# A weighted copy of 16384 token rows: 126 tokens per partition in large tiles, 256 tokens in a small tile

## The chip, the cores and the metric

The kernel runs on one core of one Trainium2 chip. The metric is the device time of one execution in microseconds; of the kernel before three runs are given. Besides, one execution was taken with the hardware profiler. Four of the core's engines matter here: VectorE (DVE in the profile) and ScalarE (ACT) compute, SyncE (SP) issues transfers, and ScalarE issues transfers too. The transfers of both are carried out by the core's sixteen DMA engines. Data lie in HBM; the on-chip memory has 128 partitions.

## The reference

Each of 16 x 1024 = 16384 tokens has a row of 512 float32 numbers and two weights. The output has two rows per token, the token's row times each weight. The expert indices are not used.

```python
batch, seq, hidden, n_experts = 16, 1024, 512, 8
k = 2

x_expanded = x[:, :, np.newaxis, :].repeat(k, axis=2)
weights = expert_weights[..., np.newaxis]
return (x_expanded * weights).astype(np.float32)
```

So 33.6 MB are read and 67.1 MB written, and each output number costs one multiplication.

## The kernel before

The tokens are dealt to 128 partitions, 128 tokens per partition, in six groups of 24, 24, 24, 24, 16 and 16 tokens per partition. Within a group each partition holds that many consecutive tokens, so that what one partition loads is one contiguous run of HBM (24 x 2 KB = 48 KB), and so is what it stores of one half group (12 x 4 KB = 48 KB).

The weights of all tokens come first, in three transfers issued by SP (line 59). A group of x is one load issued by ScalarE (`load`, line 90); the first group is loaded in six steps of 4, 4, 4, 6, 4 and 2 tokens. There are two buffers for x and two for the output. The output of a group is made in two halves; each half has a buffer of its own and one store, issued by SP (line 143).

In the first half of the first group the products are single: one instruction multiplies one row of 512 numbers in each of the 128 partitions by that partition's weight. Every third goes to ScalarE (line 110), the others to VectorE (line 116). In all other halves VectorE works in blocks of six tokens: one instruction (line 127) makes the eight rows of four tokens (or four rows where two tokens are left), with the x row repeated and the weight spread over 512 numbers, and ScalarE makes the four rows of the other two tokens singly.

What sets the order: each engine works through its instructions in order and waits on semaphores. The load of group i + 2 is issued by ScalarE after its products of group i, since it takes the buffer of group i and VectorE must also have finished with it. A half's products wait until the store that last used the output buffer (two halves earlier) has landed. The stores stand in SP's queue in the order of the halves.

Of the kernel before, what the change touches and what calls it, by code (L numbers as in the profile page):

```python
# [1 line left out]

# [4 lines left out]


@with_exitstack
def kernel(  # L10
    ctx: ExitStack,
    tc: tile.TileContext,
    x: bass.AP,
    expert_indices: bass.AP,
    expert_weights: bass.AP,
    out: bass.AP,
):
    nc = tc.nc

    batch, seq, hidden = x.shape  # L20
    k = expert_weights.shape[-1]
    P = nc.NUM_PARTITIONS
    ntok = batch * seq
    assert ntok % P == 0
    A_TOTAL = ntok // P

    f32 = mybir.dt.float32
    row = k * hidden
    TX = 24
    TO = 12  # L30
    CH = 4

    groups = [[24], [24], [24], [24], [16], [16]]
    assert sum(sum(g) for g in groups) == A_TOTAL

    xf = x.rearrange("b s h -> (b s) h")
    of = out.rearrange("b s k h -> (b s) (k h)")
    wf = expert_weights.rearrange("b s k -> (b s) k")

    w_pool = ctx.enter_context(tc.tile_pool(name="w_pool", bufs=1))  # L40
    x_pool = ctx.enter_context(tc.tile_pool(name="x_pool", bufs=2))
    o_pool = ctx.enter_context(tc.tile_pool(name="o_pool", bufs=2))

    w_tile = w_pool.tile([P, A_TOTAL * k], f32)

    def rows(of_all, done, T):
        return of_all[done * P : (done + T) * P, :].rearrange(
            "(p a) n -> p (a n)", a=T
        )

    runs = [[sum(groups[0]), 1]]
    for T in [sum(g) for g in groups[1:]]:
        if len(runs) > 1 and runs[-1][0] == T:
            runs[-1][1] += 1
        else:
            runs.append([T, 1])
    head = 0
    for T, G in runs:
        nc.sync.dma_start(
            out=w_tile[:, head * k : (head + G * T) * k].rearrange(  # L60
                "p (g n) -> p g n", g=G
            ),
            in_=wf[head * P : (head + G * T) * P, :].rearrange(
                "(g p a) n -> p g (a n)", g=G, p=P
            ),
        )
        head += G * T

    tiles = []
    done = 0  # L70
    for group in groups:
        T = sum(group)
        a0 = 0
        for n in group:
            tiles.append((done, T, a0, n))
            a0 += n
        done += T

    loaded = []

    def load(i):
        if i >= len(tiles):
            return
        done, T, a0, n = tiles[i]
        x_tile = x_pool.tile([P, TX * hidden], f32)
        src = rows(xf, done, T)
        steps = [4, 4, 4, 6, 4, 2] if i == 0 else [n]
        for e, step in enumerate(steps):
            at = sum(steps[:e])
            nc.scalar.dma_start(  # L90
                out=x_tile[:, at * hidden : (at + step) * hidden],
                in_=src[:, (a0 + at) * hidden : (a0 + at + step) * hidden],
            )
        loaded.append(x_tile)

    for i in range(2):
        load(i)
    for i, (done, T, a0, n) in enumerate(tiles):
        x_tile = loaded[i]
        outr = rows(of, done, T)  # L100
        half = n // 2
        for t in range(n):
            if t % half == 0:
                o_tile = o_pool.tile([P, TO * row], f32)
            single = i == 0 and t < half
            for kk in range(k if single or t % half % 6 > 3 else 0):
                c = (done + a0 + t) * k + kk
                o = t % half * row + kk * hidden
                if not single or c % 3 == 2:
                    nc.scalar.mul(  # L110
                        out=o_tile[:, o : o + hidden],
                        in_=x_tile[:, t * hidden : (t + 1) * hidden],
                        mul=w_tile[:, c : c + 1],
                    )
                    continue
                nc.vector.tensor_scalar(  # L116
                    out=o_tile[:, o : o + hidden],
                    in0=x_tile[:, t * hidden : (t + 1) * hidden],
                    scalar1=w_tile[:, c : c + 1],
                    scalar2=None,  # L120
                    op0=mybir.AluOpType.mult,
                )
            if not single and t % half % 6 == 0:
                c = (done + a0 + t) * k
                o = t % half * row
                m = min(CH, half - t % half)
                nc.vector.tensor_tensor(  # L127
                    out=o_tile[:, o : o + m * row].rearrange(
                        "p (t k h) -> p t k h", t=m, k=k
                    ),  # L130
                    in0=x_tile[:, t * hidden : (t + m) * hidden]
                    .rearrange("p (t h) -> p t h", t=m)
                    .unsqueeze(2)
                    .to_broadcast([P, m, k, hidden]),
                    in1=w_tile[:, c : c + m * k]
                    .rearrange("p (t k) -> p t k", t=m)
                    .unsqueeze(3)
                    .to_broadcast([P, m, k, hidden]),
                    op=mybir.AluOpType.mult,
                )  # L140
            if (t + 1) % half == 0:
                at = t // half * half
                nc.sync.dma_start(  # L143
                    out=outr[:, (a0 + at) * row : (a0 + t + 1) * row],
                    in_=o_tile[:, : (t + 1 - at) * row],
                )
        load(i + 2)

# [1 line left out]
_INS = ['x', 'expert_indices', 'expert_weights']  # L150
_OUTS = [((16, 1024, 2, 512), 'float32')]


# [23 lines left out]
```

## Time and profile before

| | |
|---|---|
| three runs | 239.81, 242.17, 242.68 us (median 242.17) |
| profiled execution | span 240.7 us; the page lists no other time for it |
| VectorE busy | 94.5 us, 38 instructions |
| ScalarE busy | 51.8 us, 81 instructions |
| moved by DMA | 100.80 MB, mean 419 GB/s |
| chain that ended last | DMA 76%, VectorE 12% of the span |

The span goes from the first to the last instruction. Stretches of the span are given with the busy time of each engine in them, the share of the sixteen DMA engines' time that was used, and the GB/s moved. A share of 1.00 means that all sixteen were busy; one engine of sixteen is 0.06. The queue q1 is SP's (weights and stores), q10 ScalarE's (loads of x), and q14 brings instructions.

### The profile page before, as it was taken

How to read it: one execution, taken by the hardware profiler on the slowest of the kernel's cores; microseconds unless marked ns; L12 is line 12 of the kernel's file. 1: busy time of each engine (PE TensorE's matmuls, PEld its weight loads, DVE VectorE, ACT ScalarE, POOL GpSimd, SP SyncE). 2: the span in 40 equal slices, each digit the busy share in tenths (PEclk: the TensorE clock that was granted, in tenths of full speed). 3: DMA queues.
4: the chain of work that ended last, by engine and by line, in shares of the span. 5: the costliest groups of instructions: out<-in, count | busy, mean ns of one | idle time of the engine just before them, and what ended most of it. 6: DMA issues, size and time to landing. Idle time of an engine off the chain costs nothing.

```text
span 240.7 us, 231 instructions
## 1 busy us (share of the span) xinstructions
DVE 94.5 (39%) x38; ACT 51.8 (22%) x81; POOL 0.2 (0%) x4
## 2 busy tenths in 40 slices
DVE  0879000002979000391067093019346005594700
ACT  0860030002553000350071170016040004043000
POOL 0000000000000000000000000000000000000000
DMA  7999999999999999999999999999999999899994
GB/s 257 427 405 451 431 404 408 498 392 408 506 392 400 515 392 392 515 402 392 482 433 392 449 436 436 436 403 490 400 427 436 427 397 438 359 436 436 436 436 180
DMA packets 4129, 100.80 MB, mean 419 GB/s; under 512 B 1184, under 2 KB 1184, under 8 KB 1312
## 3 DMA queue, kind: packets, MB, share of 16 engines
q1 hardware_dynamic: 2544, 67.24, 64.9%
q10 hardware_dynamic: 1584, 33.56, 32.9%
q14 instruction: 1, 0.01, 0.0%
HBM read 33.69 MB, written 67.11 MB: 419 GB/s over the span
## 4 chain that ended last, share of the span: by engine, by line
DMA 76%; DVE 12%; issue 4%; DVEq 1%; ACT 1%; SPq 0%; ACTq 0%
DMA out_dram<-o_tile 63%; DMA x_tile<-in_x_dram 14%; DVE o_tile L127 12%; DVEq L172 1%; ACT o_tile L110 1%; DVEq L127 0%; SPq L143 0%; ACTq L90 0%
## 5 line engine op out<-in xcount | busy, mean ns | idle before, releaser
L127 DVE TENSOR_TENSOR o_tile<-x_tile,w_tile 128x4096 f32<-128x4096 f32 (+1 forms) x22 | 87.9, 4034 | 126.0 <-DMA out_dram<-o_tile 89.5
L110 ACT ACTIVATE o_tile<-x_tile,w_tile 128x512 f32<-128x512 f32 x80 | 50.5, 709 | 164.6 <-DMA out_dram<-o_tile 124.4
L116 DVE TENSOR_SCALAR o_tile<-x_tile,w_tile 128x512 f32<-128x512 f32 x16 | 6.6, 481 | 6.7 <-DMA x_tile<-in_x_dram 6.7
L110 ACT ACT_TABLE_LOAD x1 | 1.3, 1283 | 6.7 <-DMA x_tile<-in_x_dram 6.7
L161 POOL MEMSET const-uint8-127<- 128x1 uint8 x1 | 0.1, 103 | 0.0
L161 POOL MEMSET const-bfloat16-1.0<- 128x1 bf16 x1 | 0.1, 102 | 0.0
L161 POOL MEMSET const-float32-0.0<- 128x1 f32 x1 | 0.1, 99 | 0.2 <-issue 0.2
L161 POOL MEMSET const-float32-1.0<- 128x1 f32 x1 | 0.1, 99 | 0.0
## 6 DMA issues: line engine op xcount, KB each, us to landing
out_dram<-o_tile SPq DMA_DIRECT2D x8, 6144.0 KB, 30.8
x_tile<-in_x_dram ACTq DMA_DIRECT2D x3, 6144.0 KB, 49.3
out_dram<-o_tile SPq DMA_DIRECT2D x4, 4096.0 KB, 12.5
x_tile<-in_x_dram ACTq DMA_DIRECT2D x2, 4096.0 KB, 29.0
x_tile<-in_x_dram ACTq DMA_DIRECT2D x4, 1024.0 KB, 8.6
x_tile<-in_x_dram ACTq DMA_DIRECT2D x1, 1536.0 KB, 12.8
x_tile<-in_x_dram ACTq DMA_DIRECT2D x1, 512.0 KB, 27.8
w_tile<-in_expert_weights_dram SPq DMA_DIRECT2D x1, 72.0 KB, 10.3
```

Source lines behind the costliest of these rows:

```text
L110: nc.scalar.mul(out=o_tile[:, o : o + hidden], in_=x_tile[:, t * hidden : (t + 1) * hidden], mul=w_tile[:, c : c + 1],)
L116: nc.vector.tensor_scalar(out=o_tile[:, o : o + hidden], in0=x_tile[:, t * hidden : (t + 1) * hidden], scalar1=w_tile[:, c : c + 1], scala ...
L127: nc.vector.tensor_tensor(out=o_tile[:, o : o + m * row].rearrange("p (t k h) -> p t k h", t=m, k=k), in0=x_tile[:, t * hidden : (t + m) * ...
L161: nc = _bacc.Bacc("TRN2", target_bir_lowering=False, num_devices=1)
L172: with _tile.TileContext(nc) as tc:
```

## The change

The first 256 tokens are taken out of the large tiles. The other 16128 are 126 per partition, in groups of 22, 22, 22, 22, 19 and 19; the halves have 11 and 11, or 10 and 9 tokens. A buffer for x holds 22 tokens, one for the output 11.

The 256 tokens lie in a small tile of their own. 240 of them fill partitions 32 to 91, four consecutive tokens in each, by one transfer of 60 partitions. The last 16 lie in a fifth place, in every fourth partition from 32 to 92, by one transfer of 16 partitions. This holds for their weights, for x and for the output. Their products are made on partitions 32 to 63 and 64 to 91 in turn (in the fifth place on 32 to 63 and 64 to 95, whose unused partitions two memsets have filled with zeros).

All products are single, two thirds of them on VectorE (line 112 of the new kernel) and a third on ScalarE (line 110). The small tile is loaded first, computed first and stored first. The first group's load has two parts, with the 16-partition load between them; only the first group's weights come through SP, the others through ScalarE's queue behind the first group's load. The program's order is the order in which the code stands (`manual_schedule`).

```diff
-    groups = [[24], [24], [24], [24], [16], [16]]
+    groups = [22, 22, 22, 22, 19, 19]
+    A_MAIN = sum(groups)
+    P0, NP, BAND = 32, 60, 4
+    NQ, STEP = 16, 4
+    n_band = NP * BAND
+    n_extra = n_band + NQ
...
+    def sides(t, n):
+        return (
+            t[P0 : P0 + NP, 0 : BAND * n],
+            t[P0 : P0 + NQ * STEP : STEP, BAND * n : (BAND + 1) * n],
+        )
...
+    nc.vector.memset(ew_tile[:, BAND * k :], 0.0)
+    nc.vector.memset(ex_tile[:, BAND * hidden :], 0.0)
...
+    def share(n):
+        return nc.scalar if n % 3 == 2 else nc.vector
+
+    a, b = sides(ew_tile, k)
+    nc.sync.dma_start(out=a, in_=band(wf, k))
+    nc.sync.dma_start(out=b, in_=ones(wf))
+    weights(nc.sync, 0, 1, groups[0])
+    a, b = sides(ex_tile, hidden)
+    nc.scalar.dma_start(out=a, in_=band(xf, hidden))
+    load(0, 0, 2)
+    nc.scalar.dma_start(out=b, in_=ones(xf))
+    load(0, 1, 2)
+    weights(nc.scalar, starts[1], 3, 22)
+    weights(nc.scalar, starts[4], 2, 19)
+    load(1)
+
+    for t in range(BAND + 1):
+        for p in (slice(32, 64), slice(64, P0 + NP if t < BAND else 96)):
+            for kk in range(k):
+                c = t * k + kk
+                product(share(c), p, eo_tile, c, ex_tile, t, ew_tile, c)
+    a, b = sides(eo_tile, row)
+    nc.sync.dma_start(out=band(of, row), in_=a)
+    nc.sync.dma_start(out=ones(of), in_=b)
+
+    for i, T in enumerate(groups):
...
+        for n in (T - T // 2, T // 2):
+            o_tile = o_pool.tile([P, TO * row], f32)
+            for c in range(n * k):
+                product(
...
-                nc.vector.tensor_tensor(
...
+            nc.sync.dma_start(
+                out=outr[:, at * row : (at + n) * row], in_=o_tile[:, : n * row]
+            )
+            at += n
         load(i + 2)
```

More of the change, by code (lines that the diff above doesn't have):

```diff
@@ L24 @@
     assert ntok % P == 0
-    A_TOTAL = ntok // P
     f32 = mybir.dt.float32
     row = k * hidden
-    TX = 24
-    TO = 12
-    CH = 4
-    groups = [[24], [24], [24], [24], [16], [16]]
-    assert sum(sum(g) for g in groups) == A_TOTAL
+    TX = 22
+    TO = 11
+    groups = [22, 22, 22, 22, 19, 19]
[4 more added lines that the diff above has]
+    n_extra = n_band + NQ
+    assert n_extra + A_MAIN * P == ntok
     xf = x.rearrange("b s h -> (b s) h")
@@ L40, with band, ones, rows @@
     w_pool = ctx.enter_context(tc.tile_pool(name="w_pool", bufs=1))
+    e_pool = ctx.enter_context(tc.tile_pool(name="e_pool", bufs=1))
     x_pool = ctx.enter_context(tc.tile_pool(name="x_pool", bufs=2))
     o_pool = ctx.enter_context(tc.tile_pool(name="o_pool", bufs=2))
-    w_tile = w_pool.tile([P, A_TOTAL * k], f32)
-    def rows(of_all, done, T):
-        return of_all[done * P : (done + T) * P, :].rearrange(
+    w_tile = w_pool.tile([P, A_MAIN * k], f32)
+    ew_tile = w_pool.tile([P, (BAND + 1) * k], f32)
+    ex_tile = e_pool.tile([P, (BAND + 1) * hidden], f32)
+    eo_tile = e_pool.tile([P, (BAND + 1) * row], f32)
+    def band(flat, n):
+        return flat[0:n_band, :].rearrange("(p a) n -> p (a n)", a=BAND)
+    def ones(flat):
+        return flat[n_band:n_extra, :]
+    def sides(t, n):
[3 more added lines that the diff above has]
+        )
+    def rows(flat, done, T):
+        return flat[n_extra + done * P : n_extra + (done + T) * P, :].rearrange(
             "(p a) n -> p (a n)", a=T
         )
[L51 to L59, printed above, removed]
+    def weights(eng, head, G, T):
+        lo = n_extra + head * P
+        eng.dma_start(
             out=w_tile[:, head * k : (head + G * T) * k].rearrange(
@@ L62 @@
             ),
-            in_=wf[head * P : (head + G * T) * P, :].rearrange(
+            in_=wf[lo : lo + G * T * P, :].rearrange(
                 "(g p a) n -> p g (a n)", g=G, p=P
@@ L66, with load @@
         )
[L67 to L77, printed above, removed]
+    ctx.enter_context(tc.manual_schedule())
+    nc.vector.memset(ew_tile[:, BAND * k :], 0.0)
+    nc.vector.memset(ex_tile[:, BAND * hidden :], 0.0)
+    starts = [sum(groups[:i]) for i in range(len(groups))]
     loaded = []
-    def load(i):
-        if i >= len(tiles):
+    def load(i, part=0, parts=1):
+        if i >= len(groups):
@@ L83, in load @@
             return
[L84 to L92, printed above, removed]
-            )
-        loaded.append(x_tile)
-    for i in range(2):
-        load(i)
@@ L98 @@
-    for i, (done, T, a0, n) in enumerate(tiles):
-        x_tile = loaded[i]
[L100 to L121, printed above, removed]
-                )
[L123 to L146, printed above, removed]
@@ new lines, in load, with product @@
+        T = groups[i]
+        if part == 0:
+            x_tile = x_pool.tile([P, TX * hidden], f32)
+            loaded.append(x_tile)
+        lo, hi = T * part // parts, T * (part + 1) // parts
+        nc.scalar.dma_start(
+            out=loaded[i][:, lo * hidden : hi * hidden],
+            in_=rows(xf, starts[i], T)[:, lo * hidden : hi * hidden],
+        )
+    def product(engine, p, o_tile, o, x_tile, i, w, c):
+        dst = o_tile[p, o * hidden : (o + 1) * hidden]
+        src = x_tile[p, i * hidden : (i + 1) * hidden]
+        if engine is nc.scalar:
+            engine.mul(out=dst, in_=src, mul=w[p, c : c + 1])
+        else:
+            engine.tensor_scalar(
+                out=dst,
+                in0=src,
+                scalar1=w[p, c : c + 1],
+                scalar2=None,
+                op0=mybir.AluOpType.mult,
+            )
```

11 lines of the change are left out of this document (added).

## The prediction

> **What bounds the kernel now.** I read the page first: the engines' totals, the forty slices, the DMA queues.
>
> ```profile
> span 240.7 us, 231 instructions
> DVE 94.5 (39%) x38; ACT 51.8 (22%) x81; POOL 0.2 (0%) x4
> ...
> DMA  7999999999999999999999999999999999899994
> ...
> DMA packets 4129, 100.80 MB, mean 419 GB/s; under 512 B 1184, under 2 KB 1184, under 8 KB 1312
> ...
> q1 hardware_dynamic: 2544, 67.24, 64.9%
> q10 hardware_dynamic: 1584, 33.56, 32.9%
> q14 instruction: 1, 0.01, 0.0%
> ```
>
> VectorE is busy for 39% and ScalarE for 22%; the DMA row is 9 from the second slice to the last but one. The two queues together fill 64.9 + 32.9 = 97.8% of sixteen DMA engines' span, 235.4 us of 240.7. So 5.3 us per DMA engine, on the mean, are idle, and no change that moves the same 100.80 MB at the same rate can win more than those. The question is where the 5.3 us lie. For that I cut the span into stretches.
>
> ```profile
> core 0: us, DVE busy (x) ACT busy (x) POOL busy (x), PEclk, DMA share, GB/s
> 0.00:1.70 1.70, 0.00 (x0) 0.00 (x0) 0.20 (x4) 1.00 0.00 0
> 1.70:6.00 4.30, 0.14 (x1) 0.00 (x0) 0.00 (x0) 1.00 0.99 359
> 40.00:80.00 40.00, 17.52 (x4) 10.02 (x16) 0.00 (x0) 1.00 1.00 433
> 207.00:207.60 0.60, 0.60 (x1) 0.00 (x0) 0.00 (x0) 1.00 0.01 0
> 207.60:208.80 1.20, 0.25 (x1) 0.00 (x0) 0.00 (x0) 1.00 0.57 246
> 208.80:209.20 0.40, 0.00 (x0) 0.00 (x0) 0.00 (x0) 1.00 1.53 655
> 230.00:236.00 6.00, 0.00 (x0) 0.00 (x0) 0.00 (x0) 1.00 1.01 437
> 238.20:239.40 1.20, 0.00 (x0) 0.00 (x0) 0.00 (x0) 1.00 0.06 27
> 239.40:240.70 1.30, 0.00 (x0) 0.00 (x0) 0.00 (x0) 1.00 0.00 0
> ```
>
> A stretch counts a transfer's packets where they start, so very short stretches swing between 0 and over 1, and I read them as marks of when engines start something. There are four idle places. The first 1.70 us hold no packet. The last 1.30 us hold none either (the last landing and the end of the program). From 238.20 to 239.40 the share is 0.06, which is one engine of sixteen, at 27 GB/s, which is 433 / 16: **one DMA engine works alone for 1.2 us** after the other fifteen are done. And near 208 almost nothing starts, then a burst at 208.80. Its size by subtraction: of 235.4 us busy, 0.07 lie after 238.20; 1.70 to 238.20 is 236.5 us long and holds 235.3 busy, so 1.2 us on the mean are lost there, and I put them at 208, the one place where I see engines start together.
>
> The chain of waits and the timeline tell why that gap exists.
>
> ```profile
> 170.43 30.67 DMA out_dram<-o_tile
> 201.10 0.03 issue
> ...
> 207.91 12.55 DMA out_dram<-o_tile
> ```
>
> ```profile
> 201.22 6.63 DVE L127 TENSOR_TENSOR o_tile<-x_tile,w_tile 128x4096 f32<-128x4096 f32 x2 [16.74 <-DMA out_dram<-o_tile]
> 207.91 19.69 SPq L143 DMA_DIRECT2D out_dram<-o_tile  x3
> ```
>
> A store landed at 201.10 and gave its buffer back; VectorE refilled it in 6.63 us; the next store left at 207.91. Meanwhile a single store of 4096 KB was in flight, with no load beside it: 4.19 MB at 433 GB/s is 9.7 us. The cover is 9.7 us against 6.63 plus the delay until the store begins, and a store that lands late on one engine eats the rest. So both losses, at 208 and at the end, fit one engine that lags: by 1.2 us at the end, and by at most 1.2 + 1.2 = 2.4 us without the gap, in which it could catch up.
>
> **The change, part by part.**
>
> *Which engine carries what.* Per token, 2 KB are read and 4 KB written, 6144 B, which at 433 / 16 = 27.06 GB/s take 0.227 us of one DMA engine. Before, each engine carries 16384 / 16 = 1024 tokens. After, the 128-partition transfers give it 126 x 8 = 1008, the 16-partition transfer one, and the 60-partition transfer brings 240 / n to each of the n engines on which it runs. The trace of before has no transfer of under 128 partitions, so n is open. With n = 15, fifteen engines carry 1025 tokens and one carries 1009: +0.23 us and -3.4 us. With 60 rows dealt to all 16, twelve engines would get four rows and four would get three: 1025 and 1021. I take n = 15, because 15 engines of four whole rows each is the fullest even division of 60. The lagging engine's share thus has two ends: 15 tokens less (-3.4 us) or one more (+0.23 us). I take the first, less because a row says so than because a lag that survives from the middle of the kernel to its end looks like one fixed engine, which could be spared; the other end is a rival below.
>
> By the Trainium skill, page "DMA: Bandwidth & Descriptors", section "Why a DMA increments its semaphore by 16 and not by 1", a transfer from SP or ACT uses the largest number of engines up to 16 that divides the slowest dimension, and the lowest-numbered ones: 15 for 60 partitions, the last engine left out. No run here shows it so far; by it the sum is the one made below. The same page, "Latency and other measured facts", calls engines 7 and 15 usually the slower ones, but ties this, as a guess, to transfers issued by GpSimd; both data queues here are hardware_dynamic, so by that reason the spared engine need not be the laggard. That speaks for the first rival, and by it the time would be that rival's.
>
> *The end.* If the laggard is spared, it ends at 239.4 - 3.4 = 236.0. The other fifteen ended at 238.2 with the 1.2 us gap in them; without it and with one more token, 238.2 - 1.2 + 0.2 = 237.2. They now set the end: 239.4 - 237.2 = 2.2 us less.
>
> *Does the gap at 208 close?* All products become single.
>
> ```profile
> L127 DVE TENSOR_TENSOR o_tile<-x_tile,w_tile 128x4096 f32<-128x4096 f32 x18 | 79.1, 4423 | 126.0 <-DMA out_dram<-o_tile 89.5 <-DMA x_tile<-in_x_dram 36.5
> L110 ACT ACTIVATE o_tile<-x_tile,w_tile 128x512 f32<-128x512 f32 x80 | 50.5, 709 | 164.6 <-DMA out_dram<-o_tile 124.4 <-DMA x_tile<-in_x_dram 40.2
> ...
> L116 DVE TENSOR_SCALAR o_tile<-x_tile,w_tile 128x512 f32<-128x512 f32 x16 | 6.6, 481 | 6.7 <-DMA x_tile<-in_x_dram 6.7
> ```
>
> ```profile
> 5.86 2.47 DVE L116 TENSOR_SCALAR o_tile<-x_tile,w_tile 128x512 f32<-128x512 f32 x6 [5.86 <-DMA x_tile<-in_x_dram]
> ...
> 8.00 5.14 ACT L110 ACTIVATE o_tile<-x_tile,w_tile 128x512 f32<-128x512 f32 x8
> ...
> 13.35 0.36 SPq L143 DMA_DIRECT2D out_dram<-o_tile  x1
> ```
>
> A broadcast product of eight rows took 4423 ns, 0.55 us per row; six single ones took 2.47 us, 0.41 us each. Two thirds of the rows go to VectorE: a half tile of 11 tokens has 22 rows, 15 on VectorE (6.2 us) and 7 on ScalarE (5.14 / 8 = 0.64 each, 4.5 us). Of the 10- and 9-token halves at the end, VectorE has 14 and 12 rows, 5.8 and 5.0 us. The store that covers them, alone, lasts 9.7 x 10/8 = 12.1 us or 9.7 x 9/8 = 10.9. Cover minus refill was 9.7 - 6.63 = 3.1 us; it becomes 10.9 - 5.8 = 5.1 or more. 2 us of slack are added, the gap needs 1.2: closed. Earlier, a 12-token store (14.5 us alone) covered two broadcast products (8.8 us); now 13.3 cover 6.2. Neither compute engine comes near the bound: 186 single products on VectorE x 481 ns = 89 us, 86 on ScalarE x 709 ns = 61 us.
>
> *The start.* Loads keep their queue: 0.49 MB of the band, then 5.77 MB of the first group in two parts with the 32 KB between them, then 5.77 MB of the second, 12.1 MB or 28 us at 433 GB/s. DMA is idle only if no store has come by about 30 us. VectorE now does the small tile's fourteen products first (5.8 us by the spacing above). Its band should land a little before the first load did (5.86: half the bytes), the 16 single rows behind the first half group, about 1.7 + (0.49 + 2.88) / 0.433 = 9.5 us. So the small stores leave at about 11 and the first large one at about 17 to 18, where the first left at 13.35: later, but the queue of loads still holds some 12 us. The third load leaves when the first tile is consumed, near 25, and the second is still arriving. In order on SP, the large stores stand behind the two small ones, which are ready 6 us earlier. Two memsets come on VectorE, idle until 5.86; at the size of one single product they are some 0.5 us each, and the two 16-partition loads wait for them; behind that wait stand the first group's weights on SP and the loads on ACT, which have the band's 1 us and more of work ahead of them. I take 0, and bound it by 0.5 us. The last group's weights and the second load wait on ACT for an early transfer's semaphore, as in the kernel before; behind them stand the products, whose data come at 5 us at the earliest, and in the queue ahead lie 14 us of loads.
>
> ```profile
> 0.72 5.95 ACTq L90 DMA_DIRECT2D x_tile<-in_x_dram  x7
> ```
>
> ACT's seven issues took until 6.7 us before, and seven it has now.
>
> The small weight packets (the 1184 under 512 B) stay as many within a hundred. The stretch 1.70:6.00, in which most of the old ones ran, moved 359 GB/s against 433: 4.3 x 74 / 433 = 0.7 us lost. Most now run in ACT's queue behind the first group. Between -0.7 and +0.7; I take 0, since their number is what it was.
>
> *The rest.* Instructions grow by some 150 (38 VectorE operations become about 190). Queue 14 fetched 8 KB once; I allow one more fetch on a late engine, 8 KB at 27.06 GB/s: +0.3 us; two or three on one engine would be 0.9. Row length per packet goes from 48 KB and 32 KB to 44, 40, 38 and 36; the old lengths ran at the same 433 to 437 GB/s, so 0.
> **Sum.** 240.7 - 2.2 + 0.3 = 238.8 us of span. The page gives no time for this execution besides its span, which lies within the three runs (239.81 to 242.68); their mean of 241.6 is 0.9 above it, their median 1.5. I add 0.6, less than either, since scatter from a lag on one engine should shrink when that engine has slack: **239.4 us**, 1.1% under the median.
>
> **Rivals.**
>
> *The laggard is not the engine that is spared.* For it: nothing in the profile names the engine. Against it: only that a fixed laggard could be known. The laggard may have had no gap at 208 (it was the one still at work), so closing the gap wins nothing: 240.7 + 0.2 + 0.3 = 241.2 of span, 242.0 with the mean's offset, no change.
>
> *The 60-partition transfer runs on few engines* (the slower side). Its place is the small tile's load and store; the price is (240 / n - 16) tokens x 0.227 us on those engines. With n = 12: 4 tokens, +0.9 us; with 10: 8, +1.8, about the time before; from there it decides: n = 6 gives 24, +5.4, some 245; n = 4 gives 44, +10.0, 249. For it: no such transfer in the trace. Against: 60 has the divisor 15.
>
> *Single products are dearer in the bulk than at the start*, where the 0.41 us were measured with 16 of them. The refill outgrows the cover at (10.9 - 1.2) / 14 = 0.69 us each; at 0.9 us each of the last three refills would open 2 to 3 us: about 247. Against: 478 to 487 ns is all that the 16 showed.
>
> ```profile
> L116 DVE TENSOR_SCALAR o_tile<-x_tile,w_tile x16: 478/480/487, 5.9 to 12.8; 128x512 f32<-128x512 f32 x16
> ```
>
> *More is won:* if the runs' median holds a larger lag than the profiled execution, and the start gains its 0.7: 237.5 or a little less.
>
> **How the numbers follow.** Forecast 0.62 (238.2 to 240.4); laggard not spared 0.24 (241 to 243); few engines 0.06, half of it over 2%; dear products 0.03; more won 0.05. The range from 237.6 to 242.4 holds the forecast, and most of the first rival. About 2% (237.3 and 247.0) is what a measurement of this kernel tells from no change, the three runs themselves being 1.2% apart. Faster by over 2%: most of "more won", 0.05. Slower by over 2%: half of few engines and part of dear products, 0.05. Within: 0.90.
>
> **What the profile after would show.** Right: the stretch in which one engine of sixteen works alone at the end is gone, or a share of 0.94 (fifteen of sixteen) stands shortly before the end; no stretch near the last stores without starting packets; the queues' sum at 98.5% or more of a span near 238.8. First rival: a share of 0.06 for over a microsecond at the end still. Few engines: shares of n / 16 at the end, for several microseconds. Dear products: the single products' mean well over 481 ns, and stores that wait for VectorE with the DMA row below 9. I would be wrong altogether if the DMA rate itself changed: less than 433 GB/s in the stretch from 40 to 80 us.

## The result, and the profile after

The changed kernel takes 252.99 us (median of four runs, 252.58 to 254.55) against 241.03 (239.81 to 242.68) before: ratio 1.0516, 95% interval 1.0462 to 1.057, slower. I had predicted 239.4 us, and 0.05 for slower by over 2%. One thing has to be said for the numbers that follow: the runs of one kernel can lie up to 14 us apart, so for each experiment all its times are given or described, and a ratio compares, of each kernel's runs taken together, only those within about 1.5% of its fastest.

The page of the changed kernel, the lines that answer to those shown of before:

```profile
span 251.5 us, 394 instructions
DVE 76.1 (30%) x188; ACT 55.9 (22%) x87; POOL 0.2 (0%) x4
...
DMA  5999899999999869999997999999999999989991
GB/s 215 401 400 467 380 451 423 416 387 395 423 444 408 387 222 387 451 395 444 444 437 289 423 427 427 443 459 448 392 427 434 432 426 421 429 351 489 400 463 76
DMA packets 3876, 100.82 MB, mean 401 GB/s; under 512 B 1289, under 2 KB 1289, under 8 KB 1321
...
q1 hardware_dynamic: 2086, 67.13, 63.6%
q10 hardware_dynamic: 1787, 33.66, 31.9%
q14 instruction: 3, 0.02, 0.0%
```

The bytes are the same, VectorE has less to do (76.1 us busy against 94.5) and ScalarE 4 us more (55.9 against 51.8), yet the span is 10.8 us longer. The queues' sum is 63.6 + 31.9 = 95.5% of 251.5, 240.2 us busy per DMA engine, where before had 235.4; idle are 11.3 us, where before had 5.3. So of the 10.8 us **4.8 are packets that took longer, and 6.0 are engines with nothing to do.** The GB/s row shows holes (222, 289, and a shallow one of 351); in the page of before the lowest slice between the first and the last has 359.

The stretches around the deepest hole, and the end (engines' busy time, the granted clock, DMA share, GB/s):

```profile
30.00:84.00 54.00, 6.03 (x15) 4.40 (x7) 0.00 (x0) 1.00 1.00 414
84.00:88.40 4.40, 3.48 (x9) 3.58 (x6) 0.00 (x0) 1.00 0.78 338
88.40:91.80 3.40, 2.55 (x7) 0.81 (x2) 0.00 (x0) 1.00 0.31 133
91.80:98.00 6.20, 0.00 (x0) 0.00 (x0) 0.00 (x0) 1.00 1.06 356
98.00:133.00 35.00, 11.19 (x29) 8.80 (x14) 0.00 (x0) 1.00 1.00 430
133.00:136.00 3.00, 0.87 (x3) 0.00 (x0) 0.00 (x0) 1.00 0.89 300
...
246.60:248.80 2.20, 0.00 (x0) 0.00 (x0) 0.00 (x0) 1.00 0.31 134
```

A share of 0.31 is five engines of sixteen: from 88.4 to 91.8 eleven are idle and five work, and so again after 246.6. From 30 to 84 all are busy, but at 414 GB/s, where the kernel before moved 431 in the same stretch; from 91.8 to 98, when all start again together, they are busy at 356.

The timeline shows why the eleven had nothing to do:

```profile
54.19 6.03 DVE L112 TENSOR_SCALAR o_tile<-x_tile,w_tile 128x512 f32<-128x512 f32 x15 [24.51 <-DMA out_dram<-o_tile]
60.29 31.05 SPq L162 DMA_DIRECT2D out_dram<-o_tile  x2
84.82 4.40 ACT L110 ACTIVATE o_tile<-x_tile,w_tile 128x512 f32<-128x512 f32 x7 [26.37 <-DMA out_dram<-o_tile]
84.92 6.03 DVE L112 TENSOR_SCALAR o_tile<-x_tile,w_tile 128x512 f32<-128x512 f32 x15 [24.69 <-DMA out_dram<-o_tile]
91.03 0.36 ACTq L101 DMA_DIRECT2D x_tile<-in_x_dram  x1
```

A store left at 60.29; the next could leave only when VectorE had refilled the other buffer, and that began at 84.82, when the store that held the buffer had landed. The trace keeps a record of each of the sixteen engines reporting its share of a transfer. For that store (second half of the first group), and for the last store, these are the times at which the engines reported, in order (us):

```
                                  1st     2nd     7th    11th    12th    15th    16th
store that frees the buffer
  before                        67.71   67.84   68.02   68.09   68.12   68.18   69.05
  after                         73.67   75.05   75.26   75.55   84.37   84.73   84.79
last store
  before                       238.29  238.30  238.36  238.38  238.40  238.47  239.82
  after                        246.73  246.76  246.84  246.90  249.03  250.41  250.42
```

**Five engines report nine microseconds after the eleventh.** A landing is that of the slowest engine: the refill waits for it, the eleven finish the one store that is left (at 88.8 by the same records) and run dry until 91.8. This repeats, smaller, at 134 and 223. The records do not name the engines; that the same five lag each time is inferred from their number.

### The profile page after: what moved, and what is told of

The parts are those of the page before. It is cut to its first block, busy times and chain, and to the rows that moved or that the text cites. A ratio compares the mean times of both kernels' runs of the same rounds, so it can differ in the third digit from the quotient of the medians.

```text
span 251.5 us, 394 instructions
## 1 busy us (share of the span) xinstructions
DVE 76.1 (30%) x188; ACT 55.9 (22%) x87; POOL 0.2 (0%) x4
## 3 DMA queue, kind: packets, MB, share of 16 engines
q1 hardware_dynamic: 2086, 67.13, 63.6%
q10 hardware_dynamic: 1787, 33.66, 31.9%
## 4 chain that ended last, share of the span: by engine, by line
DMA 65%; DVE 16%; another core or an unknown queue 10%; issue 1%; ACTq 0%; DVEq 0%; SPq 0%
DMA out_dram<-o_tile 61%; DVE o_tile L112 15%; DMA ex_tile<-in_x_dram 5%; ACTq L128 0%; DVE eo_tile L112 0%; DVEq L112 0%; DVEq L191 0%; ACTq L101 0%; SPq L162 0%
## 5 line engine op out<-in xcount | busy, mean ns | idle before, releaser
L112 DVE TENSOR_SCALAR o_tile<-x_tile,w_tile 128x512 f32<-128x512 f32 x172 | 69.2, 481 | 148.6 <-DMA out_dram<-o_tile 145.6
L112 DVE TENSOR_SCALAR eo_tile<-ex_tile,ew_tile 32x512 f32<-32x512 f32 (+1 forms) x14 | 6.4, 475 | 6.9 <-DMA ex_tile<-in_x_dram 6.8
L110 ACT ACTIVATE eo_tile<-ex_tile,ew_tile 32x512 f32<-32x512 f32 (+1 forms) x6 | 4.3, 719 | 3.5 <-DMA ex_tile<-in_x_dram 3.5
```

Of the source, the lines that this page charges most:

```text
L110: engine.mul(out=dst, in_=src, mul=w[p, c : c + 1])
L112: engine.tensor_scalar(out=dst, in0=src, scalar1=w[p, c : c + 1], scalar2=None, op0=mybir.AluOpType.mult,)
```

## The experiments

Theories after the result. **R**: the groups of 22 and 19 give row lengths and pitches in HBM (the pitch is the distance from one partition's row to the next) at which stores are slow. **U**: the small tile's uneven transfers put the engines out of step. **S**: the single products, or the start (first group in two parts, weights behind it), are at fault. Later **W**: whatever makes an engine lag, the time is lost where a refill waits for its landing with a single store as the others' cover, that is, as the only work left to them. The diffs are cut to the lines that matter; where group sizes change, the buffers' sizes and the weights' transfers follow.

**1. The kernel before with the group sizes alone.**

```diff
-    groups = [[24], [24], [24], [24], [16], [16]]
+    groups = [[22], [22], [22], [22], [20], [20]]
...
-        steps = [4, 4, 4, 6, 4, 2] if i == 0 else [n]
+        steps = [4, 4, 4, 4, 4, 2] if i == 0 else [n]
```

> The kernel before with groups of 22, 22, 22, 22, 20 and 20 tokens (128 per partition, no small tile, block products kept). Theory R (the row lengths and pitches of 44 and 88 KB make the stores slow): 249 to 254 us, with store packets stretched and part of the DMA engines lagging as in the changed kernel. Theory U (the small tile's uneven transfers put the engines out of step) and theory S (the single products, or the start with two-part load and weights behind it, are at fault): 240 to 243 us.

Measured: 252.42, 254.32, 255.17, and once 243.29 us. Neither the small tile nor the single products are needed for the loss, which fits R. That one run in four was free of it does not: the same addresses then went at nearly full rate.

**2. The small tile even.** The changed kernel, the 256 tokens in one 64-partition transfer each way (the 16-partition transfers and the memsets go).

```diff
-    P0, NP, BAND = 32, 60, 4
+    P0, NP, BAND = 32, 64, 4
...
-    nc.scalar.dma_start(out=a, in_=band(xf, hidden))
+    nc.scalar.dma_start(
+        out=ex_tile[P0 : P0 + NP, : BAND * hidden], in_=band(xf, hidden)
+    )
...
-    nc.scalar.dma_start(out=b, in_=ones(xf))
...
```

> The changed kernel with the 256 tokens in one 64-partition transfer each way (partitions 32 to 95, four tokens each) instead of 60 and 16. Theory U: the time falls to 238 to 242 us, because all sixteen engines carry the same. Theories R and S: it stays at 250 to 254.

Measured: eight of ten runs at 241.94 to 243.99, two at 250.22 and 250.97; ratio 1.0081 (1.0051 to 1.0111). With nearly all else as in the changed kernel, 22-token groups go at the old rate in most runs, so R alone falls; and the loss still comes, in two runs here and in experiment 1, without any uneven transfer, so U alone falls too.

**3. The kernel before with single products.**

```diff
-            single = i == 0 and t < half
+            single = True
```

> The kernel before with all products single, every third on ScalarE. Theory S in the part of the products: 249 us or more. Theories R and U: 239 to 242, the refill of a half falling from 8.8 to about 6.6 us, and the DMA engines as before.

Measured: 241.14 to 243.16, ratio 1.0041 (1.0002 to 1.008). The single products do not make the loss.

**4. The small tile late.** Loaded after the last large load, computed and stored ahead of the last group.

```diff
-    a, b = sides(ex_tile, hidden)
-    nc.scalar.dma_start(out=a, in_=band(xf, hidden))
     load(0, 0, 2)
-    nc.scalar.dma_start(out=b, in_=ones(xf))
...
         load(i + 2)
+        if i == 3:
+            a, b = sides(ex_tile, hidden)
+            nc.scalar.dma_start(out=a, in_=band(xf, hidden))
+            nc.scalar.dma_start(out=b, in_=ones(xf))
```

> The changed kernel with the small tile loaded after the last large load and computed and stored ahead of the last group. Theory U in its form 'an early lead of one engine and lag of others is carried through the kernel': 238 to 242, the engines landing together until 200 us. If uneven transfers cost wherever they stand, or theory R or S holds: 250 to 254.

Measured: all ten runs within 241.15 to 241.97, ratio 1.0032 (1.0004 to 1.0059). The uneven transfers cost next to nothing when they stand late.

**5 to 7. Other row lengths, the small tile early as in the changed kernel.** Seven groups of 18; groups of 24 and 15 stored in pieces of 8 and 7; groups of 22 and 19 stored in pieces of 8, 7 and 6.

```diff
-    groups = [22, 22, 22, 22, 19, 19]
+    groups = [18] * 7
```

> The changed kernel with seven groups of 18 tokens (rows of 36 KB in loads and stores), the small tile early as it was. Theory G (it takes both: the 22-token groups' addresses, and engines out of step early): 239 to 243 us, no stretched store packets in 30 to 80 us. Theory U alone (engines out of step slow each other whatever the rows): 249 to 254.

```diff
-    groups = [22, 22, 22, 22, 19, 19]
+    groups = [24, 24, 24, 24, 15, 15]
...
-        for n in (T - T // 2, T // 2):
+        for n in {24: (8, 8, 8), 15: (8, 7)}[T]:
```

> The changed kernel with groups of 24, 24, 24, 24, 15 and 15 tokens, stored in pieces of 8 (or 8 and 7) tokens so that the buffers fit: loads and pitch of the kernel before (48 KB, 96 KB in the output), small tile early. Theory G: 239 to 243. Theory U alone: 249 to 254.

```diff
-        for n in (T - T // 2, T // 2):
+        for n in {22: (8, 7, 7), 19: (7, 6, 6)}[T]:
```

> The changed kernel with its own groups of 22 and 19 and its loads, but stored in pieces of 8, 7 and 7 (7, 6 and 6) tokens: pitch of 88 KB kept, store rows of 32 and 28 KB. If the pitch in HBM is what makes out-of-step engines slow: 248 to 254 in most runs. If it is the store rows' length of 44 KB, or stores and loads of one length taking turns: 239 to 243.

Measured: 246.02 to 259.76; 245.99 to 250.79 (ratio 1.0236, 1.0157 to 1.0314); 245.73 to 249.83 (1.0312, 1.0196 to 1.0429). All three lose, whatever the length, though for the second and third the intervals reach down below 2%. In the second, loads and pitch are those of the kernel before. Theory G, as I had by then put it (it takes the 22-token addresses and an early lag together), falls with them. The third has three of its four runs where the pitch alone would put them, but the second loses at the old pitch too. Groups of 18 with two buffers are the worst of all.

The three do not lose in the same way. By the queues' shares the first's engines are busy for 240.5 us and idle for 17.5 of its 258.0; the second's 237.9 and 6.3 of 244.2; the third's 241.3 and 6.7 of 248.0. Beside the 235.4 and 5.3 of before, the second and third lose mainly by longer packets, which theory W does not explain.

**8. The kernel before with an uneven first load** (0.49 MB that nothing uses).

```diff
+    nc.scalar.dma_start(
+        out=d_tile[32:92, :],
+        in_=xf[0:240, :].rearrange("(p a) n -> p (a n)", a=4),
+    )
```

> The kernel before, whose first transfer is now a load of 60 partitions (240 tokens, 8 KB each) into a tile that nothing uses, 0.49 MB more on 15 of 16 engines. Theory G: the groups of 24 bear it, 241 to 243 us (1.1 us more than before). Theory U alone: 248 or more, as soon as the first transfer is uneven.

Measured: 242.32 to 244.83, ratio 1.0108 (1.003 to 1.0186), some 2.6 us, of which 1.1 are the load's own by the forecast. Three of the four runs lie where theory G had them. An uneven first transfer is not enough.

**9 to 11. One part of the start undone at a time**: the small tile stored late; the first group's loads ahead of the small tile's (which is then computed and stored after the first group); the first group in six steps as before.

```diff
-    a, b = sides(eo_tile, row)
-    nc.sync.dma_start(out=band(of, row), in_=a)
-    nc.sync.dma_start(out=ones(of), in_=b)
-
     for i, T in enumerate(groups):
+        if i == 5:
+            a, b = sides(eo_tile, row)
+            nc.sync.dma_start(out=band(of, row), in_=a)
+            nc.sync.dma_start(out=ones(of), in_=b)
```

> The changed kernel with the small tile loaded and computed first as it is, but stored ahead of the last group. Theory A (the small early stores, uneven among the engines and mixed with the loads, put them out of step): 240 to 243 us. Theory B (the early loads do it, before any store): 249 to 254.

```diff
+    load(0, 0, 2)
+    load(0, 1, 2)
     a, b = sides(ex_tile, hidden)
     nc.scalar.dma_start(out=a, in_=band(xf, hidden))
-    load(0, 0, 2)
     nc.scalar.dma_start(out=b, in_=ones(xf))
-    load(0, 1, 2)
...
```

> The changed kernel with the first group's two loads ahead of the small tile's, which is computed and stored between the first and the second group. Theory B in the form that the very first transfer must not be uneven: 240 to 244. Theory A or an uneven transfer anywhere in the first 40 us: 247 to 254.

```diff
-    load(0, 0, 2)
+    for lo, hi in ((0, 4), (4, 8), (8, 12)):
+        step(lo, hi)
     nc.scalar.dma_start(out=b, in_=ones(xf))
-    load(0, 1, 2)
+    for lo, hi in ((12, 16), (16, 20), (20, 22)):
+        step(lo, hi)
```

> The changed kernel with the first group loaded in steps of 4, 4, 4, 4, 4 and 2 tokens as in the kernel before, instead of two parts. Theory C (the long packets of the two-part load are stretched in the first 10 us and leave some engines a microsecond behind): 240 to 244. Theories A and B: 249 to 254.

Measured: 241.00 to 247.22 (six of ten under 242); 241.12 to 242.48; 240.59 to 244.37. The ratios are 1.0028 (0.9987 to 1.0069), 1.0026 (0.9998 to 1.0054), 1.0018 (0.9983 to 1.0053). **With each of the three the loss is gone in all or most runs**, in the first not in all: its profiled run is the one of 247.22 us, with 235.6 us busy and 9.8 idle (of 245.4), a loss by idle engines alone, without longer packets. Each met the interval of its own theory, A in six of ten runs, B in all and C in nine, so none of the three parts is enough by itself. I infer that the loss needs an early lag that the combination sets up nearly always, and other starts now and then. One reservation: so far as is recorded, the changed kernel was not run on the chip of experiments 9 to 12, so a share of that chip in the good times is not excluded. The page of the second:

```profile
span 239.6 us, 393 instructions
...
q1 hardware_dynamic: 2086, 67.13, 64.9%
q10 hardware_dynamic: 1787, 33.66, 33.4%
```

The same packets are now 64.9 + 33.4 = 98.3% of 239.6: 235.5 us busy, 4.1 idle. Both losses are gone together.

**12. More cover, groups of 18.** Four buffers of 6 tokens instead of two of 9; everything else as in experiment 5.

```diff
-    TO = 9
+    TO = 6
...
-    o_pool = ctx.enter_context(tc.tile_pool(name="o_pool", bufs=2))
+    o_pool = ctx.enter_context(tc.tile_pool(name="o_pool", bufs=4))
...
-        for n in (T - T // 2, T // 2):
+        for n in (6, 6, 6):
```

> The kernel with seven groups of 18, early small tile, with the output in four buffers of 6 tokens instead of two of 9. Theory W (the time goes where a refill waits for the slowest engine's landing while the other engines run dry, since one store is all their cover): with three stores in flight as cover, 240 to 246 against the 255.6 with two buffers. If the stretched packets themselves are the loss: 250 to 258.

Measured: 241.96 to 245.54, ratio 1.0115 (1.0039 to 1.0192), where two buffers gave 246 to 260, on another chip. The trace shows the cover at work: refills waited until 118.5, 151.2 and 184.0 us for two engines that reported seven microseconds after the other fourteen (111.5, 144.4 and 177.2), and meanwhile (112 to 119, 145 to 152, 178 to 185) the engines moved 428, 439 and 430 GB/s. Idle are 5.8 us in all, against 17.5 in the profiled run with two buffers. W is borne out; the next pair takes out the difference of chips.

**13 and 14. More cover in the changed kernel itself, and the changed kernel again beside it**, on one chip.

```diff
-    TO = 11
+    TO = 5
...
-    o_pool = ctx.enter_context(tc.tile_pool(name="o_pool", bufs=2))
+    o_pool = ctx.enter_context(tc.tile_pool(name="o_pool", bufs=4))
...
-        for n in (T - T // 2, T // 2):
+        for n in {22: (5, 5, 4, 4, 4), 19: (5, 5, 5, 4)}[T]:
```

> The changed kernel with its output in four buffers of 5 tokens (stores of 5, 5, 4, 4, 4 and of 5, 5, 5, 4 tokens) instead of two of 11; loads, groups and the early small tile as they are. Theory W (a refill waits for the slowest engine's landing, with one store as the others' cover): 240 to 246 us, the idle share falling to that of the kernel before. If the stretched packets and the lag alone are the loss: 250 to 254.

> The changed kernel unaltered, beside the run with four buffers on the same chip. If the loss belongs to the kernel: 252 to 255 us in all or nearly all runs. If it belongs to the chip or the hour of the first measurement: 239 to 243 in part of them, as the variants with one part undone gave.

Measured: with four buffers all ten runs at 242.72 to 243.97, ratio 1.0083 (1.0048 to 1.0119). Unaltered: 254.59, 250.58, 250.33, and once 242.68. So the loss belongs to the kernel, in seven of eight runs taken of it; and where the others need not wait for a laggard, it is gone. In its one run without the loss the changed kernel took 0.7% more than the 241.03 of before: most of the 5.2% of the result is this loss, and not the other work of the changed program. With four buffers the page reads

```profile
span 240.7 us, 446 instructions
...
q1 hardware_dynamic: 4390, 67.14, 65.1%
q10 hardware_dynamic: 1787, 33.66, 33.4%
```

237.1 us busy and 3.6 idle, against 240.2 and 11.3; and the stretches that had the hole:

```profile
30.00:84.00 54.00, 15.17 (x38) 9.23 (x14) 0.00 (x0) 1.00 1.01 429
84.00:98.00 14.00, 3.28 (x9) 1.95 (x3) 0.00 (x0) 1.00 1.02 435
```

Here too a lag was there at first: fifteen engines reported the first two large stores by 27.70 and 34.14 us and the last one at 39.67 and 45.55, 12.0 and 11.4 us later. The refill waited for it (VectorE went on at 39.79), but the others had a load and further stores to work on: 435 GB/s from 30 to 40 us, 411 from 40 to 50. Of that load one engine reported at 39.49 and the other fifteen from 50.55 on. If it is the same engine, which the records do not say, it was not slow, but had taken the load ahead of the stores. From 85 us on, where the changed kernel had its deepest hole, the lag is 2 us or less behind the middle engine, so that four buffers may also keep a lag from growing; experiment 12 alone shows them covering one that stayed. They also mean shorter stores (5 tokens): two buffers with stores of 8 tokens still lost (6 and 7), and two with stores of 5 were not run.

The repeat of the changed kernel shows the mechanism at its barest. Its page and the same hole:

```profile
span 252.8 us, 394 instructions
...
q1 hardware_dynamic: 2086, 67.13, 62.5%
q10 hardware_dynamic: 1787, 33.66, 32.3%
```

```profile
30.00:84.00 54.00, 6.14 (x16) 4.40 (x7) 0.00 (x0) 1.00 1.01 430
...
88.40:91.80 3.40, 2.80 (x8) 1.07 (x2) 0.00 (x0) 1.00 0.09 40
91.80:98.00 6.20, 0.00 (x0) 0.00 (x0) 0.00 (x0) 1.00 1.05 349
```

Its store that frees the buffer was reported by fifteen engines at 73.77 to 77.89, and by the last at 85.04. Here up to 84 us nearly no rate is lost (430 GB/s), **one single engine** lags by seven microseconds, and a share of 0.09 is what is left of sixteen engines while they wait for it. Idle in all: 252.8 x (1 - 0.948) = 13.1 us.

**15. More cover in the kernel before.** Four buffers of 6 tokens, a store per quarter of a group.

```diff
-    TO = 12
+    TO = 6
...
-    o_pool = ctx.enter_context(tc.tile_pool(name="o_pool", bufs=2))
+    o_pool = ctx.enter_context(tc.tile_pool(name="o_pool", bufs=4))
...
-        half = n // 2
+        half = n // 4
```

> The kernel before with its output in four buffers of 6 tokens (a quarter of a group, 4 in the last two groups) instead of two of 12, stores as many tokens long. Theory W says that its own scatter (239.9 to 247 us) comes from refills that wait for a lagging engine: then the runs should lie close together, 239.5 to 241.5, with none over 243. If the scatter has another cause: 240 to 246 as before.

Measured: twelve runs at 241.35 to 243.07, median 241.75, while the kernel before, beside it on the same chip, went from 239.85 to 252.64 with a median of 241.83 and five of sixteen runs over 243.07; ratio 1.0044 (1.0014 to 1.0074). One run went 0.07 us over the 243 that I had set, and the median missed my interval by 0.25. The scatter is gone, as W says. The kernel before had a loss as large as the changed one's in one run, the only one over 248 us among all ninety taken of it; of that run there is no profile, so that it lost its time by the same wait is not shown. What it does not give is a lower time in the good runs, so no version here beats the kernel before at its best.

## Why the prediction was wrong, point by point

*The step that failed: "2 us of slack are added, the gap needs 1.2: closed."* The mechanism at that place was the right one, a store that lands late on one engine and a refill that waits for it; the sizes were not. I set the slack (cover minus refill, 5.1 us and 7.1 earlier) against the lag that I read from the end of one execution, at most 2.4 us. Even the trace of before has a larger one: the store whose landing let VectorE go on at 177.86 us was reported by fifteen engines from 173.63 to 174.38 and by the last at 177.74, 3.4 us later. After the change the lag at the store of 84 us was nine, more than any slack in the sum, and gaps opened at 91, 134 and 223 us. The refill itself was as forecast (6.03 us for 15 products where I had 6.2; the forecast for the halves at the end, 5.8 and 5.0, is met by 5.63 and 4.84), and so was the price of a product:

```profile
L112 DVE TENSOR_SCALAR o_tile<-x_tile,w_tile 128x512 f32<-128x512 f32 x172 | 69.2, 481 | 148.6 <-DMA out_dram<-o_tile 145.6
```

481 ns as in the kernel before, so the rival of dear products falls. I had no rival in which the engines drift apart, although each refill has one store as its cover; that is the case that came.

*"The old lengths ran at the same 433 to 437 GB/s, so 0."* Wrong as a bound for the whole: 4.8 us of longer packets, and the sign that I had set for being wrong altogether came, 410 GB/s from 40 to 80 us (423 in the repeat). But not for the reason that the step left out, the row length: experiments 2, 4, 10 and 11 run the same rows at the old rate (235.3 to 235.7 us busy in their profiled runs). In the changed kernel the long packets come with the lag and with the common restarts. By the trace's packets, store packets of 4 KB and more that took over 60 ns longer than their size gives, out of all, in slices of ten microseconds:

```
                        30-40    40-50    50-60    60-70    70-80   90-100
after                   15/48    10/43    15/48    11/44    15/78    17/45
after, taken again       3/48     2/48     3/44     3/48     3/83    16/38
loads ahead (no. 10)     0/50     0/48     1/46     0/70    0/152     0/35
```

In the first row some fifteen in ten microseconds would be three packets of each of five engines (if loads and stores of 1.67 us take turns, an engine starts three stores in ten). In the second they would be one engine's three. The sums fit: from 30 to 80 us the long ones took 37.7 us more than their size gives in the first row, 7.5 for each of five engines, and 7.3 in the second, where one lags by seven. The last column is the restart after the gap. Why just some engines get the long store packets I cannot say; that is open.

*"+0.23 us and -3.4 us", with n = 15.* Right as to n. The trace's semaphore record of the first 60-partition load of weights has one increment at 1.30 us, before any data packet (the first starts at 1.71), and fifteen from 2.06 to 3.28. That agrees with the Trainium skill, "DMA: Bandwidth & Descriptors", "Why a DMA increments its semaphore by 16 and not by 1", by which the sequencer at once writes the increments of the engines that a transfer doesn't use. So the rival of few engines falls.

*"If the laggard is spared."* The tail was not gone, where it can be seen at all. In experiment 10, with no large loss, the last store was reported by one engine at 235.26, by the next ones at 236.57 to 236.97, and by the last at 238.55: the engine that leads by 1.3 us has the smaller share, I infer, and others trail the group by up to 1.6. The end of that kernel,

```profile
234.00:236.50 2.50, 0.00 (x0) 0.00 (x0) 0.00 (x0) 1.00 0.62 265
236.50:238.40 1.90, 0.00 (x0) 0.00 (x0) 0.00 (x0) 1.00 0.09 39
```

still has the tail that I had meant to be gone. That was the sign and about the time of the first rival, at 0.24: 242.0, where experiments 4 and 10, without the large loss, came to 241.1 to 242.5. Its mechanism is not shown: by the forecast's sum the spared engine should lead by 3.6 us, and whether it lost 2.3 of them because it was the laggard, or for want of work, can't be told from records that name no engine.

*The baseline, a term that was mis-sized.* The 2.2 us were to be won from an execution of 240.7 us of span. Most runs of the kernel before are better than that: 62 of the 86 with a recorded span lie under 240.7, like 240.04 us of time and 238.0 of span. I infer that they had not paid the lag's 2.4 us, so that there was next to nothing to win; none of them has a profile. The same pairs put 1.9 to 2.2 us between time and span (after: 253.27 and 251.5), where I added 0.6. With 2 us the forecast span of 238.8 would have been 240.8 us of time.

*The start.* The first large store left at 20.82, not at 17 to 18, and the third load at 29.77, not near 25, since the second half of the first group's data came at 23.6. The engines were not idle for it (a share of 0.99 from 1.70 to 30 us), though they moved 401 GB/s there, where before moved 419. Three instruction fetches instead of the two that I allowed, 0.3 us each on some engine: too small to see.

*What settles it and what does not.* Shown: the loss is gone with more cover, in the changed kernel itself and beside it on one chip (13, 14); and with more cover refills waited seven microseconds for a laggard while the engines kept their rate (12). Shown with the reservation on the chip: it is gone or rarer with any of three parts of the start undone (9, 10, 11), with the same rows and the same small tile. Shown too: an uneven tile is neither needed (1) nor enough (4, 8). Open: which state of the engines in the first 25 us starts the drift, why it keeps growing, and why packets grow longer with little idle time in experiments 6 and 7; kernels that lag by as much at 20 us (2.4 in experiment 11 between first and last) came through unharmed.

## What to carry to other kernels

A transfer lands when the slowest of sixteen DMA engines is done (84.79 us above, where the eleventh was done at 75.55), so with two buffers and one store as cover, a single engine that falls some microseconds behind stops the other fifteen; three or more transfers in flight made the times of both kernels here steady. Read the slack between a landing and the next issue not against one profile's lag, but against what a bad run can have, and look at several runs' spans before taking a profile's gaps as time to be won. An edit that reorders the first transfers can decide the rate 50 us later, so undo the parts of a start one by one before blaming sizes or engines.

## What was not expected

A lag comes back. In the repeat of the changed kernel the last engine (I take it to be the same one) reported the first-half stores of the second, third and fourth group 12.6, 9.8 and 8.4 us after the fifteenth (103.73 against 91.17, 144.11 against 134.36, 183.09 against 174.68), and the second-half store of the third only 4.9 us after it (166.03 against 161.16): as I read it, the gaps let it catch up, and each stage with loads beside stores set it back. A common restart is itself dear: 349 to 356 GB/s for the six microseconds after 91.8, against 433, 1.1 to 1.2 us each. And the kernel before, taken as the steady reference, has such runs in it: 252.64 us in one of ninety, 23 of them over 243.07, and none over that in twelve with four smaller buffers.
